# One array tile per chunk for the recurrence heads, and a re-ordered normalization at the end of the first feed-forward block

## The chip, the cores and the metric

The kernel runs on 1 core of one Trainium2 chip. The metric is the device time of one execution in microseconds (us). Engines are named as in the profile: PE is TensorE (PEld its weight loads), DVE is VectorE, ACT is ScalarE, POOL is GpSimd, SP issues DMAs.

## The reference

Two layers run over 128 context tokens and 1024 latent tokens (1152 in all, D = 1024). Layer 0 is attention beside a gated convolution, then a gated ConvFFN; layer 1 is a two-way gated linear recurrence (HGRN2), then a ConvFFN. All products are fp32. What matters here:

```
xp = _layer_norm(ALPHA * xp + gt2_p * fp, ln2_g[l], ln2_b[l])     # end of each layer, the same for xs
...
z = (h @ w_in).astype(F32)                                        # next layer, h = x*(1+scale)+shift
q, i, g, f_fw, f_bw = jnp.split(z, 5, axis=-1)
...
scores = jnp.einsum('bhtk,bhsk,bhtsk->bhts', qb, kb, decay)       # per head, within a chunk
o = o_inter + jnp.einsum('bhts,bhsv->bhtv', scores, vb)
S_new = exp(b_last) * S + jnp.einsum('bhsk,bhsv->bhkv', kb * jnp.exp(b_last - b), vb)
```

So each token's row gets a mean and a variance, is normalized, scaled and shifted, and then enters the recurrence's input projection; there, each of 8 heads builds decayed keys and queries.

## The kernel before, in words

Tokens lie in 9 tiles t of 128 rows, taken from t = 8 down to 0, and in 3 chunks c of 384 columns (tiles 3c to 3c+2), taken 2, 1, 0. A product in fp32 precision is three matmuls of a high and a low half (mm3, L93 to L95): high is a rounded copy (ACT), low the remainder (value minus high).

All engines run the order in which the code is written (one manual schedule over all engines); each engine takes its instructions in that order and waits at semaphores, which the tile framework sets from what overlaps in a tile.

**End of a feed-forward block** (ffn_down, loop at L1408). For each t PE makes two halves of 12 matmuls of 512 columns into a bank pair psw. Then DVE multiplies by the gate rows (L1421), adds into y[t] and sums it (L282), ACT squares with a sum (L285). That is ln_sums; its second part, end(), is: DVE L288, POOL's power -0.5 (L289), DVE L290, ACT L291, which writes the normalized y[t]. settle(t+1) calls end() of the tile before between the two halves of tile t.

For layer 0, tail0 puts jobs into a list todo when a chunk's three tiles are normalized: 4 jobs for chunk 2, 3 for chunk 1; the fifth of these rows of work and chunk 0's are left to the start of the next layer (later0). A job is ln_out for two 128-blocks: 6 PE transposes (L320) into two banks psl, one evacuated by DVE (L328), one by ACT (L325), both into hts with scale and shift; ACT then writes the high half (L335) and DVE or POOL the low half (L336) of the next layer's input, in turn. Jobs are taken after each half of the products. The dictionary pre adds the next layer's first weights: at t = 7 two DMAs, at t = 4, 2 and 0 one split each (ACT L108, then DVE L109).

**Start of the recurrence.** PE runs the first projections (psp, 384 columns) with later0's five jobs between them (psl's role is taken by pss there).

**Heads** (L1579 on). A head's four arrays KBF, QAB, QAF, KBB of 1152 columns are one tile X. For 7 levels and 3 chunks, 21 items: mixed_keys (ACT L1624) copies km out of X for the item after; level makes 3 products per item (PE L1635, shown as 6 rows) from km and X, then multiplies parts of X in place, one half on POOL and one on DVE (both L1641), and DVE puts the scores in place by a mask (L1643). Between items, fill(n) runs steps of 3 projection matmuls for the next head. Head 7 has no next head, so there is less to fill with.

Lines that the prediction's steps touch: L282 to L291, L320 to L336, L1399 to L1426, L1446 to L1456, L108, L109, L1568 to L1573, L1583, L1592 to L1598, L1621 to L1644.

Of the kernel before, what the change touches and what calls it, by code (L numbers as in the profile page):

```python
# [80 lines left out]
def build(tc, ins, outs, consts):  # L81
# [197 lines left out]
    def ln_sums(z, p2, small, other=None, junk=None):  # L279
# [7 lines left out]
        def end():  # L287
            nc.vector.tensor_scalar(mv[:, 3:4], mv[:, 2:3], 1.0 / D, EPS, op0=ALU.mult, op1=ALU.add)  # L288
            nc.gpsimd.tensor_tensor(mv[:, 4:5], mv[:, 3:4], mhalf[:, 0:1], op=ALU.pow)  # L289
            nc.vector.tensor_tensor(mv[:, 5:6], mv[:, 1:2], mv[:, 4:5], op=ALU.mult)  # L290
            nc.scalar.activation(z, z, AF.Identity, bias=mv[:, 5:6], scale=mv[:, 4:5])  # L291
        return end
# [13 lines left out]
    def ln_affine(xn, gb, out, dst, eng=None):  # L306

        for cols, e in eng or ((slice(0, D), (nc.gpsimd, nc.gpsimd)),):
            e[0].tensor_tensor(out[:, cols], xn[:, cols], gb[:, 0, cols], op=ALU.mult)  # L309
            e[1].tensor_tensor(out[:, cols], out[:, cols], gb[:, 1, cols], op=ALU.add)  # L310
            nc.sync.dma_start(dst[:, cols], out[:, cols])

# [969 lines left out]
    def ffn_down(l, xsrc, mod_list, dw, tail, pre):  # L1282
        with ExitStack() as st:
# [114 lines left out]
            todo, behind, end = [], [], None  # L1398
            def settle(t):  # L1399

                nonlocal behind
                if end:
                    end()
# [4 lines left out]
            for t in range(NT - 1, -1, -1):  # L1408
# [6 lines left out]
                if todo:  # L1415
                    todo.pop(0)()
                products(ps[:, 1, :], gi, t, [NU - 2, NU - 1])
                if todo:
                    todo.pop(0)()
                p2 = ps.rearrange("p a b -> p (a b)")  # L1420
                nc.vector.tensor_tensor(p2, p2, rows[:, cond_of(t), :], op=ALU.mult)  # L1421
                end = ln_sums(y[t], p2, lp)
                if t in pre:
                    pre[t]()
            settle(0)
# [6 lines left out]
    def tail0(t, y, gb, x1_tile, bank, lp, todo):  # L1432
# [5 lines left out]
        if t % 3 == 0:  # L1438
# [13 lines left out]
            now = [lambda f=f: f(bank, tmp) for f in fs[:n]]  # L1452
            if c:
                todo.append(lambda: None)
            now[2:2] = [lambda: None] * (c == 2)
            todo += now  # L1456
# [36 lines left out]
    m32 = gp.tile([P, 4, NTOK], I32, tag="X", name="m32").rearrange("p a b -> p (a b)")[:, :7 * P].rearrange(  # L1493
# [33 lines left out]
    def scan_ap(X, a0, a1, c0, n, h):  # L1527
# [3 lines left out]
                       [list(base.ap[0]), [2 * h, n // (2 * h)], [(a1 - a0) * NTOK + h, 2], [1, h]])  # L1531
# [7 lines left out]
    class Head:  # L1539
# [42 lines left out]
        def begin(self):  # L1582
            self.X = persistent("X", [P, 4, NTOK])  # L1583
# [8 lines left out]
        def arrays(self, c):  # L1592
            X, fb, q, cols = self.X, self.fb, self.q[c], colsof(c)
            nc.scalar.activation(X[:, 0:4:3, cols], fb[:, :, cols], AF.Identity, bias=one, scale=-1.0)
            nc.gpsimd.tensor_tensor(X[:, QAF, cols], q, fb[:, 0, cols], op=ALU.mult)
            nc.vector.tensor_tensor(X[:, QAB, cols], q, fb[:, 1, cols], op=ALU.mult)
            kk = self.kk[c] = wtile("kk")
            nc.vector.tensor_tensor(kk, X[:, KBF, cols], X[:, KBB, cols], op=ALU.add)  # L1598
# [22 lines left out]
        def mixed_keys(self, lv, c):  # L1621
# [3 lines left out]
                           scan_ap(self.X, KBF, KBB, c * 384, 384, hh))  # L1625

        def level(self, lv, c):
            X, cols = self.X, colsof(c)
# [4 lines left out]
            for q3 in range(3):  # L1633
                c0 = c * 384 + q3 * P
# [490 lines left out]
```

## Time and profile before

| | |
|---|---|
| median of 3 runs | 3256.94 us (3255.2 to 3258.32) |
| the profiled execution | 3256.72 us, span of its instructions 3254.9 us |
| PE busy | 3136.4 us, 96% of the span |
| DVE, ACT, POOL busy | 2247.9 (69%), 1288.9 (40%), 1422.9 us (44%) |
| mean granted TensorE clock | 0.99 |

The last product of the first feed-forward block's end starts at 1448.84 us and the last of later0's transposes ends at 1537 us; the heads' items run from 1583 to 2311 us. Times within the span are us from its start. A row of the timeline is: start, duration, engine, line, operation, output from input, shapes, how many, and in brackets the idle time of the engine before it and what ended it. A row of the view of waits is: engine, tile and line that waited, for whom, and then us in total, times, longest.

### The profile page before, as it was taken

Reading aid. Unit: us, or ns where it says so; the run is one execution under the profiler, and the core shown is the slowest. Engines: PE = TensorE matmul, PEld = TensorE weight load, DVE = VectorE, ACT = ScalarE, POOL = GpSimd, SP = SyncE. Lnnn points to the kernel's source line nnn. Section 1 sums busy time; section 2 is a strip of 40 time slices with the busy share of each in tenths; the row PEclk is TensorE's granted clock in tenths of the full one; section 3 lists DMA queues with packets and bytes.
Section 4 is the critical chain, followed back from the end, with each engine's and each line's share of the span. In section 5 each row is a group of like instructions: output and inputs, shape, how many; then the busy total and the mean of one; then the engine's idle time right before and its main releaser. Section 6 shows DMA issues by size and latency. Waiting matters only on the chain. (4 is left out here: it accounts for less than half of the span.)

```text
span 3254.9 us, 48740 instructions
## 1 busy us (share of the span) xinstructions
PE 3136.4 (96%) x19231; PEld 2906.1 (89%) x19231; DVE 2247.9 (69%) x3117; ACT 1288.9 (40%) x2162; POOL 1422.9 (44%) x1011
## 2 busy tenths in 40 slices
PE   7999999899999999998999999999999999999997
PEld 5999888789999998877999999999779999998886
DVE  6778888448988976674466666655556889675356
ACT  4411998333333333115433334333443433335112
POOL 6821242335444534562244333333424545444465
PEclk9999999999999999999999999999999999999999
DMA  7142000322222335541322222211331222225452
GB/s 221 35 136 91 1 1 1 129 85 67 95 91 88 91 119 188 171 154 64 99 83 76 65 68 80 62 50 43 111 122 55 87 91 91 69 82 185 154 169 83
DMA packets 267476, 305.42 MB, mean 94 GB/s; under 512 B 19587, under 2 KB 200015, under 8 KB 267248
## 3 DMA queue, kind: packets, MB, share of 16 engines
q1 hardware_dynamic: 266160, 299.49, 29.0%
q8 instruction: 152, 2.49, 0.3%
q0 software_dynamic: 1088, 2.82, 0.3%
q14 instruction: 76, 0.62, 0.1%
HBM read 237.84 MB, written 64.42 MB: 93 GB/s over the span
## 5 line engine op out<-in xcount | busy, mean ns | idle before, releaser
L1099 POOL TENSOR_TENSOR wlo<-S,whi 128x512 fp32r<-128x512 f32 x152 | 243.1, 1613 | 251.9 <-ACT whi L1098 251.3
L109 POOL TENSOR_TENSOR wlo<-wraw,whi 128x1024 fp32r<-128x1024 f32 x78 | 198.0, 2541 | 203.4 <-ACT whi L108 203.2
L93 PE MATMUL psd<-whi,s 128*128 128x512 f32 x720 | 284.0, 394 | 0.9 <-DVE u L1243 0.9
L95 PE MATMUL psd<-whi,s 128*128 128x512 f32 x720 | 284.0, 394 | 0.0
L94 PE MATMUL psd<-wlo,s 128*128 128x512 f32 x720 | 284.0, 394 | 0.0
L1641 POOL TENSOR_TENSOR X<-X,tot 128x384 f32<-128x384 f32 x144 | 181.4, 1260 | 226.8 <-PE pss L1635 173.7
L1127 DVE SCALAR_TENSOR_TENSOR t<-u,fcw,t 128x1156 f32<-128x1156 f32 x152 | 266.2, 1768 | 13.5 <-ACT t L1122 10.8
L95 PE MATMUL psq<-T,wlo 128*128 128x290 f32 x912 | 271.0, 297 | 0.0
L94 PE MATMUL psq<-T,whi 128*128 128x290 f32 x912 | 270.5, 297 | 0.0
L93 PE MATMUL psq<-T,whi 128*128 128x290 f32 x912 | 270.3, 296 | 0.0
L1099 POOL TENSOR_TENSOR wlo<-wraw,whi 128x512 fp32r<-128x512 f32 x114 | 182.2, 1599 | 173.1 <-ACT whi L1098 157.3
L108 ACT ACTIVATE whi<-wraw 128x1024 fp32r<-128x1024 f32 x130 | 136.8, 1054 | 291.2 <-DMA wraw<-in_ffn_w_down_dram 107.0
L1098 ACT ACTIVATE whi<-S 128x512 fp32r<-128x512 f32 x152 | 92.9, 627 | 323.2 <-DVE S L1077 249.0
L1357 DVE TENSOR_TENSOR y<-y,psd 128x512 f32<-128x512 f32 x144 | 98.0, 684 | 171.9 <-PE psd L95 171.3
L213 DVE SCALAR_TENSOR_TENSOR macc<-mraw,sil,macc 128x512 f32<-128x512 f32 x182 | 191.7, 1092 | 7.1 <-DMA mraw<-in_w_mod_dram 7.1
L93 PE MATMUL psu<-h,whi 128*128 128x388 f32 (+1 forms) x504 | 175.0, 348 | 12.1 <-DVE sc L639 6.9
L1641 DVE TENSOR_TENSOR X<-X,tot 128x384 f32<-128x384 f32 x144 | 102.1, 709 | 113.1 <-PE pss L1635 75.1
L94 PE MATMUL psu<-h,whi 128*128 128x388 f32 (+1 forms) x504 | 174.4, 346 | 2.5 <-POOL h L428 2.5
L1635 PE MATMUL pss<-X,km 128*128 128x128 f32 x1008 | 153.2, 289 | 23.7 <-ACT km L1624 10.3
L93 PE MATMUL psp<-s,whi 128*128 128x384 f32 x480 | 174.7, 364 | 0.0
L95 PE MATMUL psu<-h,wlo 128*128 128x388 f32 (+1 forms) x504 | 173.2, 344 | 0.0
L94 PEld LDWEIGHTS psq<-T,whi 128*128 128x128 f32 x912 | 172.5, 189 | 0.0
(442 smaller groups left out, 10005.2 us busy)
## 6 DMA issues: line engine op xcount, KB each, us to landing
wraw<-in_ffn_w_up_dram SPq DMA_DIRECT2D x88, 512.0 KB, 3.8
mraw<-in_w_mod_dram SPq DMA_DIRECT2D x104, 256.0 KB, 2.8
sraw<-sd SPq DMA_DIRECT2D x40, 578.0 KB, 4.6
wraw<-in_ffn_w_down_dram SPq DMA_DIRECT2D x44, 512.0 KB, 4.1
sd<-t SPq DMA_DIRECT2D x36, 578.0 KB, 3.0
wraw<-in_hgrn_w_in_dram SPq DMA_DIRECT2D x40, 512.0 KB, 4.1
mraw<-in_w_mod_dram SPq DMA_DIRECT2D x28, 512.0 KB, 4.0
wraw<-in_attn_w_in_dram SPq DMA_DIRECT2D x18, 512.0 KB, 3.8
```

The source lines that it names most:

```text
L93: mm(ps, l[0], r[0], start=start, stop=False)
L94: mm(ps, l[0], r[1], start=False, stop=False)
L95: mm(ps, l[1], r[0], start=False, stop=stop)
L108: nc.scalar.activation(hi[:, :n], raw[:, :n], AF.Copy)
L109: (eng or nc.gpsimd).tensor_tensor(lo[:, :n], raw[:, :n], r32(hi[:, :n]), op=ALU.subtract)
L213: nc.vector.scalar_tensor_tensor(acc[:, cond, :], raw, sil[:, cond, k:k + 1], acc[:, cond, :], op0=ALU.mult, op1=ALU.add)
L1098: nc.scalar.activation(hi, src, AF.Copy)
L1099: nc.gpsimd.tensor_tensor(lo, src, r32(hi), op=ALU.subtract)
L1127: nc.vector.scalar_tensor_tensor(t, u[:, :, c0:c0 + HO], taps(p + NF * x)[c0], t, op0=ALU.mult, op1=ALU.add)
L1357: nc.vector.tensor_tensor(y[t][:, cols], y[t][:, cols], ps, op=ALU.add)
L1635: mm(ps[:, q3 * P:(q3 + 1) * P], km[:, q3 * P:(q3 + 1) * P], scan_ap(X, QAB, QAF, c0, P, hh), start=True, stop=True)
L1641: eng.tensor_tensor(x, x, t4[:, :, :, 1 - half].unsqueeze(3).to_broadcast([P, 2, nb, hh]), op=ALU.mult)
```

## The change

It does three things. (1) ln_sums can return its second part in two, factor (L288, L289) and apply (the rest). In settle, factor comes first, then waiting low halves, then a job's transposes and evacuations, then apply, then a weight split, then that job's high and low half. The second place for a job is after the second half of the products, where both evacuations are on ACT, the high half comes after the square, and the low half waits for the next settle. So there is one job per place, and a free place ahead of each chunk's first. The splits of t = 4, 2 and 0 move from behind the sums of tiles 4, 2 and 0 to behind apply of tiles 3, 1 and 0. (2) The low halves of these seven jobs are all on POOL. (3) X becomes three tiles X0, X1, X2 of 384 columns, one per chunk.

```diff
--- before.py
+++ after.py
@@ ln_sums @@
-    def ln_sums(z, p2, small, other=None, junk=None):
+    def ln_sums(z, p2, small, other=None, junk=None, two=False):
...
-        def end():
+        def factor():
             nc.vector.tensor_scalar(mv[:, 3:4], mv[:, 2:3], 1.0 / D, EPS, op0=ALU.mult, op1=ALU.add)
             nc.gpsimd.tensor_tensor(mv[:, 4:5], mv[:, 3:4], mhalf[:, 0:1], op=ALU.pow)
+
+        def apply():
             nc.vector.tensor_tensor(mv[:, 5:6], mv[:, 1:2], mv[:, 4:5], op=ALU.mult)
             nc.scalar.activation(z, z, AF.Identity, bias=mv[:, 5:6], scale=mv[:, 4:5])
-        return end
+        return (factor, apply) if two else lambda: (factor(), apply())
+    def ln_pair(c, xns, l, i, bank, tmp, hT, segs, k0):
+
+
+        (cond, h0, n), = segs
+        o, box = hgb[:, l, i, cond], {}
+
+        def front(alone):
+            box["t"] = t2 = tmp()[:, :768].rearrange("p (a b) -> p a b", b=384)
+            for k in (k0, k0 + 1):
+                ps = bank()
+                for q in range(3):
+                    nc.tensor.transpose(ps[:, q * P:(q + 1) * P], xns[q][:, k * P:(k + 1) * P], ident)
+                if k % 2 or alone:
+                    nc.scalar.activation(t2[:, k - k0, :], ps[:, :n], AF.Identity, bias=o[:, 1, k:k + 1],
+                                         scale=o[:, 0, k:k + 1])
+                else:
+                    nc.vector.tensor_scalar(t2[:, k - k0, :], ps[:, :n], o[:, 0, k:k + 1], o[:, 1, k:k + 1],
+                                            op0=ALU.mult, op1=ALU.add)
+
+        def high():
+            nc.scalar.activation(hT[0].ks(k0, 2, h0, n), box["t"], AF.Copy)
+
+        def low():
+            nc.gpsimd.tensor_tensor(hT[1].ks(k0, 2, h0, n), box["t"], r32(hT[0].ks(k0, 2, h0, n)), op=ALU.subtract)
+        return front, high, low
@@ ffn_down @@
-            todo, behind, end = [], [], None
+            todo, behind, end, lows = [], [], None, []
...
                 if end:
-                    end()
+                    end[0]()
+                    for f in lows:
+                        f()
+                    lows.clear()
+                    job = todo.pop(0) if todo else None
+                    if job:
+                        job[0](False)
+                    end[1]()
+                    if t + 1 in pre:
+                        pre[t + 1]()
+                    if job:
+                        job[1]()
+                        job[2]()
...
-                if todo:
-                    todo.pop(0)()
                 products(ps[:, 1, :], gi, t, [NU - 2, NU - 1])
-                if todo:
-                    todo.pop(0)()
+                job = todo.pop(0) if todo else None
+                if job:
+                    job[0](True)
                 p2 = ps.rearrange("p a b -> p (a b)")
                 nc.vector.tensor_tensor(p2, p2, rows[:, cond_of(t), :], op=ALU.mult)
-                end = ln_sums(y[t], p2, lp)
+                end = ln_sums(y[t], p2, lp, two=True)
+                if job:
+                    job[1]()
+                    lows.append(job[2])
+            settle(0)
+            for t in (1, 0):
                 if t in pre:
                     pre[t]()
-            settle(0)
@@ tail0 @@
-            now = [lambda f=f: f(bank, tmp) for f in fs[:n]]
             if c:
-                todo.append(lambda: None)
-            now[2:2] = [lambda: None] * (c == 2)
-            todo += now
+                todo += [None] + [ln_pair(c, y[3 * c:3 * c + 3], 0, 1, bank, tmp, state["h"], hsegs(c, False), 2 * a)
+                                  for a in range(n)]
@@ heads @@
-                       [list(base.ap[0]), [2 * h, n // (2 * h)], [(a1 - a0) * NTOK + h, 2], [1, h]])
+                       [list(base.ap[0]), [2 * h, n // (2 * h)], [(a1 - a0) * 384 + h, 2], [1, h]])
...
-            self.X = persistent("X", [P, 4, NTOK])
+            self.X = [persistent(f"X{c}", [P, 4, 384]) for c in range(3)]
...
-                           scan_ap(self.X, KBF, KBB, c * 384, 384, hh))
+                           scan_ap(self.X[c], KBF, KBB, 0, 384, hh))
...
-            X, cols = self.X, colsof(c)
+            X = self.X[c]
...
-                x = X[:, arrs, cols].rearrange("p a (n s r) -> p a n s r", s=2, r=hh)[:, :, :, half, :]
+                x = X[:, arrs, :].rearrange("p a (n s r) -> p a n s r", s=2, r=hh)[:, :, :, half, :]
```

The same replacement of X by X[c] stands in arrays, state_at, flip and output. Nothing on the SP queue changes its place.

**VectorE in the end of the first feed-forward block**, from the sum of tile 4 (y_12166) to the gate product of tile 3. hts is a job's evacuated transposes, h_13784 and s_13405 are low halves of the next layer's input, wlo a weight's low half, bmv the statistics of a tile. Before:

```order
L282 SCALAR_TENSOR_TENSOR y_12166,bmv<-psw,y_12166 128x1024
L284 TENSOR_SCALAR bmv<-bmv 128x1
L109 TENSOR_TENSOR wlo<-wraw,whi 128x1024
L288 TENSOR_SCALAR bmv<-bmv 128x1
L290 TENSOR_TENSOR bmv<-bmv 128x1
L328 TENSOR_SCALAR hts<-psl,hgb 128x384 x2
L336 TENSOR_TENSOR s_13405<-hts,s_13404 128x2x384
L1421 TENSOR_TENSOR psw<-psw,rows 128x1024
L282 SCALAR_TENSOR_TENSOR y_12167,bmv<-psw,y_12167 128x1024
```

With the change, the same stretch and one tile more:

```order
L282 SCALAR_TENSOR_TENSOR y_12166,bmv<-psw,y_12166 128x1024
L284 TENSOR_SCALAR bmv<-bmv 128x1
L288 TENSOR_SCALAR bmv<-bmv 128x1
L331 TENSOR_SCALAR hts<-psl,hgb 128x384
L292 TENSOR_TENSOR bmv<-bmv 128x1
L1461 TENSOR_TENSOR psw<-psw,rows 128x1024
L282 SCALAR_TENSOR_TENSOR y_12167,bmv<-psw,y_12167 128x1024
L284 TENSOR_SCALAR bmv<-bmv 128x1
L288 TENSOR_SCALAR bmv<-bmv 128x1
L292 TENSOR_TENSOR bmv<-bmv 128x1
L109 TENSOR_TENSOR wlo<-wraw,whi 128x1024
L1461 TENSOR_TENSOR psw<-psw,rows 128x1024
```

The weight split has moved from ahead of a tile's own statistics to ahead of the next tile's gate product, the evacuation of a job stands ahead of the second part of the normalization, and the low half has left this engine.

**GpSimd in the same stretch**, from the first power of -0.5 after the last whole split to the last tile's. Before:

```order
L289 TENSOR_TENSOR bmv<-bmv,mhalf 128x1 x3
L336 TENSOR_TENSOR h_13784<-hts,h_13783 128x2x384
L289 TENSOR_TENSOR bmv<-bmv,mhalf 128x1 x2
L336 TENSOR_TENSOR s_13405<-hts,s_13404 128x2x384
L289 TENSOR_TENSOR bmv<-bmv,mhalf 128x1
L336 TENSOR_TENSOR h_13784<-hts,h_13783 128x2x384
L289 TENSOR_TENSOR bmv<-bmv,mhalf 128x1
L336 TENSOR_TENSOR s_13405<-hts,s_13404 128x2x384
```

With the change:

```order
L289 TENSOR_TENSOR bmv<-bmv,mhalf 128x1 x4
L338 TENSOR_TENSOR h_13784<-hts,h_13783 128x2x384
L289 TENSOR_TENSOR bmv<-bmv,mhalf 128x1
L338 TENSOR_TENSOR h_13784<-hts,h_13783 128x2x384
L338 TENSOR_TENSOR s_13405<-hts,s_13404 128x2x384
L289 TENSOR_TENSOR bmv<-bmv,mhalf 128x1
L338 TENSOR_TENSOR s_13405<-hts,s_13404 128x2x384
L289 TENSOR_TENSOR bmv<-bmv,mhalf 128x1
L338 TENSOR_TENSOR h_13784<-hts,h_13783 128x2x384
L289 TENSOR_TENSOR bmv<-bmv,mhalf 128x1
L338 TENSOR_TENSOR h_13784<-hts,h_13783 128x2x384
L338 TENSOR_TENSOR s_13405<-hts,s_13404 128x2x384
```

Seven low halves stand there instead of four, three of them directly behind a tile's power.

**PE in the first head**, where the products of the second item (chunk 1) follow six of the projection's matmuls; the engines named are those whose semaphores the row waits for. Before:

```order
L93 MATMUL psp_14729<-h00_13783,whi_14564 128x384
L94 MATMUL psp_14729<-h10_13784,whi_14564 128x384
L95 MATMUL psp_14729<-h00_13783,wlo_14565 128x384
L1635 MATMUL pss_14735<-X_14568,km_14712 128x128 [waits Pool_49]
L1635 MATMUL pss_14735<-X_14568,km_14712 128x128 x2
```

With the change:

```order
L93 MATMUL psp_14731<-h00_13783,whi_14564 128x384
L94 MATMUL psp_14731<-h10_13784,whi_14564 128x384
L95 MATMUL psp_14731<-h00_13783,wlo_14565 128x384
L1676 MATMUL pss_14737<-X1_14569,km_14714 128x128 [waits PE_49,Activation_49]
L1676 MATMUL pss_14737<-X1_14569,km_14714 128x128 x2
```

The place is the same; the wait for GpSimd, which multiplies in chunk 2 at that time, is gone, and what is left is the wait for this chunk's own km.

## Rows read from the trace of the kernel before

**Rows 1.** The page's first part: busy time, share of the span and instructions of PE.
```profile
PE 3136.4 (96%) x19231; PEld 2906.1 (89%) x19231; DVE 2247.9 (69%) x3117; ACT 1288.9 (40%) x2162; POOL 1422.9 (44%) x1011
```
**Rows 2.** Waits of PE from 1440 to 1537 us, the end of the first feed-forward block and the start of the recurrence.
```profile
PE psl L320 <- DVE hts L328: 4.8, 2, 4.3
PE psl L320 <- ACT y L291: 3.2, 2, 2.3
PE pss L320 <- ACT psw L285: 2.0, 1, 2.0
PE pss L320 <- ACT y L291: 1.5, 1, 1.5
PE psl L320 <- ACT hts L325: 1.2, 2, 0.8
```
**Rows 3.** Busy time by stretch in the same place: length, then busy us and instructions of PE, PEld, DVE, ACT, POOL, the granted clock, DMA share, GB/s.
```profile
1470.00:1490.00 20.00, 15.10 (x74) 11.88 (x72) 9.60 (x19) 9.30 (x14) 3.47 (x4) 0.95 0.00 1
1490.00:1510.00 20.00, 16.94 (x66) 13.41 (x66) 9.42 (x17) 10.20 (x13) 4.78 (x4) 0.79 0.09 27
```
**Rows 4.** Groups of instructions by line and shape from 1449 to 1537 us: busy us, mean ns of one, idle before.
```profile
L1421 DVE TENSOR_TENSOR psw<-psw,rows 128x1024 f32<-128x1024 f32 x9 | 11.0, 1224 | 1.0 <-PE psw L95 1.0
L285 ACT ACTIVATE psw<-y,bmv 128x1024 f32<-128x1024 f32 x9 | 10.1, 1119 | 32.9 <-DVE bmv L284 32.9
L289 POOL TENSOR_TENSOR bmv<-bmv,mhalf 128x1 f32<-128x1 f32 x9 | 4.9, 543 | 43.1 <-DVE bmv L288 43.1
L336 POOL TENSOR_TENSOR h<-hts,h 128x768 fp32r<-128x768 f32 x2 | 3.7, 1852 | 8.8 <-ACT h L335 8.8
L109 DVE TENSOR_TENSOR wlo<-wraw,whi 128x1024 fp32r<-128x1024 f32 x3 | 3.7, 1226 | 6.9 <-ACT whi L108 6.9
```
**Rows 5.** The timeline around PE's longest wait in that place, one engine's rows after the other (DVE, then PE).
```profile
1481.71 0.96 DVE L336 TENSOR_TENSOR h<-hts,h 128x768 fp32r<-128x768 f32 x1 [2.22 <-ACT h L335]
...
1487.59 1.23 DVE L109 TENSOR_TENSOR wlo<-wraw,whi 128x1024 fp32r<-128x1024 f32 x1 [2.31 <-ACT whi L108]
...
1489.67 0.67 DVE L328 TENSOR_SCALAR hts<-psl,hgb 128x384 f32<-128x384 f32 x1
...
1490.40 0.90 PE L320 MATMUL psl<-ident,y 128*128 128x128 f32 x3 [4.34 <-DVE hts L328]
```
**Rows 6.** Busy time by stretch, columns as in Rows 3: one middle head's period, then the first and the second part of head 7's items.
```profile
1678.00:1777.00 99.00, 97.03 (x647) 95.71 (x647) 66.53 (x122) 39.04 (x70) 42.10 (x31) 1.00 0.26 83
2262.00:2280.00 18.00, 13.89 (x79) 12.68 (x78) 12.03 (x28) 6.72 (x13) 7.39 (x6) 0.91 0.15 51
2280.00:2312.00 32.00, 26.28 (x176) 23.11 (x174) 23.26 (x37) 12.39 (x24) 20.97 (x17) 1.00 0.32 100
```
**Rows 7.** Waits of PE from 1580 to 2262 us, heads 0 to 6.
```profile
PE pss L1635 <- ACT km L1624: 8.1, 7, 1.2
PE pss L1635 <- POOL X L1641: 3.8, 8, 1.7
PE pss L1635 <- DVE X L1641: 1.6, 5, 0.3
```
**Rows 8.** Waits of PE from 2262 to 2312 us, head 7.
```profile
PE pss L1635 <- POOL X L1641: 5.9, 6, 1.3
PE pss L1635 <- ACT km L1624: 2.3, 4, 1.1
PE pss L1635 <- DVE X L1641: 0.5, 1, 0.5
```
**Rows 9.** The view of tile X, POOL's products in it: count, duration ns min/median/max, first and last start, shapes.
```profile
L1641 POOL TENSOR_TENSOR X<-X,tot x144: 837/1254/2017, 1595.2 to 2310.2; 128x384 f32<-128x384 f32 x144
```
**Rows 10.** The timeline of PE in head 7: the last projection matmul ahead of an item's products and those products, once with a wait and once without.
```profile
2284.65 0.34 PE L95 MATMUL psp<-s,wlo 128*128 128x384 f32 x1
2286.25 0.94 PE L1635 MATMUL pss<-X,km 128*128 128x128 f32 x6 [1.26 <-POOL X L1641]
2286.94 0.42 PE L93 MATMUL psp<-s,whi 128*128 128x384 f32 x1
...
2298.37 0.34 PE L95 MATMUL psp<-s,wlo 128*128 128x384 f32 x1
2298.55 0.83 PE L1635 MATMUL pss<-X,km 128*128 128x128 f32 x6
2299.14 0.42 PE L93 MATMUL psp<-s,whi 128*128 128x384 f32 x1
```
**Rows 11.** The timeline at head 0's first item: two runs of the same five small products of two SBUF tiles on DVE, and POOL's first product in X.
```profile
1582.34 1.32 DVE L1610 TENSOR_TENSOR tot<-tot 128x192 f32<-128x192 f32 x5
1584.36 2.25 DVE L1610 TENSOR_TENSOR tot<-tot 128x192 f32<-128x192 f32 x5
...
1584.64 1.19 POOL L1641 TENSOR_TENSOR X<-X,fb 128x384 f32<-128x384 f32 x1 [18.58 <-PE pss L1635]
```
**Rows 12.** The timeline at the end of head 0: a power on POOL, POOL's next instruction, and the DVE instruction that waited for the power.
```profile
1660.63 0.86 POOL L1697 TENSOR_TENSOR ss<-ss,mhalf 128x3 f32<-128x3 f32 x1 [6.92 <-DVE ss L1696]
1661.47 0.99 POOL L1595 TENSOR_TENSOR X<-q,fb 128x384 f32<-128x384 f32 x1
...
1661.53 0.56 DVE L1699 TENSOR_TENSOR on<-pss,ss 128x384 f32<-128x384 f32 x1 [0.98 <-POOL ss L1697]
```

More of the change, by code (lines that the diff above doesn't have):

```diff
@@ L1492, in build @@
     masks = gs.tile([P, 7, P], U8, name="masks")
-    m32 = gp.tile([P, 4, NTOK], I32, tag="X", name="m32").rearrange("p a b -> p (a b)")[:, :7 * P].rearrange(
+    m32 = gp.tile([P, 4, 384], I32, tag="X0", name="m32").rearrange("p a b -> p (a b)")[:, :7 * P].rearrange(
         "p (a b) -> p a b", b=P)
@@ L1592, in arrays @@
         def arrays(self, c):
[L1593 to L1596, printed above, removed]
+            X, fb, q, cols = self.X[c], self.fb, self.q[c], colsof(c)
+            nc.scalar.activation(X[:, 0:4:3, :], fb[:, :, cols], AF.Identity, bias=one, scale=-1.0)
+            nc.gpsimd.tensor_tensor(X[:, QAF, :], q, fb[:, 0, cols], op=ALU.mult)
+            nc.vector.tensor_tensor(X[:, QAB, :], q, fb[:, 1, cols], op=ALU.mult)
             kk = self.kk[c] = wtile("kk")
-            nc.vector.tensor_tensor(kk, X[:, KBF, cols], X[:, KBB, cols], op=ALU.add)
+            nc.vector.tensor_tensor(kk, X[:, KBF, :], X[:, KBB, :], op=ALU.add)
         def totals(self, c):
@@ L1633, in level @@
             for q3 in range(3):
-                c0 = c * 384 + q3 * P
-                mm(ps[:, q3 * P:(q3 + 1) * P], km[:, q3 * P:(q3 + 1) * P], scan_ap(X, QAB, QAF, c0, P, hh),
+                mm(ps[:, q3 * P:(q3 + 1) * P], km[:, q3 * P:(q3 + 1) * P], scan_ap(X, QAB, QAF, q3 * P, P, hh),
                    start=True, stop=True)
@@ L1649, in state_at @@
                 return self.S0[:, dr, :]
-            return self.X[:, KBB if dr else KBF, t * P:(t + 1) * P]
+            return self.X[t // 3][:, KBB if dr else KBF, t % 3 * P:(t % 3 + 1) * P]
         def flip(self, dr, c):
@@ L1654, in flip @@
             for q3 in range(3):
-                t = 3 * c + q3
                 nc.tensor.transpose(pt[:, q3 * P:(q3 + 1) * P],
-                                    self.X[:, KBB if dr else KBF, t * P:(t + 1) * P], ident)
+                                    self.X[c][:, KBB if dr else KBF, q3 * P:(q3 + 1) * P], ident)
             kb = wtile("kb")
@@ L1681, in output @@
             po = pst()
-            X, V = self.X, shared["V"]
+            X, V = self.X[c], shared["V"]
             for q3 in range(3):
                 t = 3 * c + q3
-                cols = slice(t * P, (t + 1) * P)
+                cols = slice(q3 * P, (q3 + 1) * P)
                 o = po[:, q3 * P:(q3 + 1) * P]
```

## The prediction

> **What bounds it now.** The page's first part comes first: PE is busy for 3136.4 of 3254.9 us [rows 1], so that only stretches in which PE stands, or runs at its lower clock, can give time back. The view of PE's waits, taken by stretch, then shows which of them lie where the diff works. The reader is to see three places. From 1440 to 1537 us PE stands 12.7 us in all (4.8 + 3.2 + 2.0 + 1.5 + 1.2), each time ahead of transposes [rows 2]; the timeline shows the longest of these waits, 4.34 us, with VectorE's rows ahead of it [rows 5]; and right behind it the clock granted to TensorE averages 0.79 over 20 us [rows 3], a mixture of its two levels, 2.4 and 1.2 GHz, after PE had stood. In heads 0 to 6 PE waits 5.4 us for POOL's and DVE's products in X and 8.1 us for km [rows 7]. In head 7, which has little to fill with, it waits 5.9 and 0.5 us for X and 2.3 us for km [rows 8]. A middle head is dense, 97.03 us busy in 99 [rows 6]; head 7 is not, 13.89 in 18 and 26.28 in 32.
>
> **End of the feed-forward block, wait by wait.** The largest, 4.8 us, is for the evacuation L328. In the timeline it stands on VectorE behind the weight split L109, which itself idled 2.31 us for ACT's half; L328 then runs 0.67 us and PE resumes [rows 5]. Afterwards the evacuation stands ahead of both the second part of the normalization and the split. I take all 4.8 us as gone. The 3.2 us for y are waits of a job's transposes that came one after the other in the same pause; a job now stands at least 12 matmuls later, some 2.4 us (74 PE instructions take 15.10 us [rows 3], 0.20 each), against a longest wait of 2.3: gone too. Of the 1.2 us for ACT's evacuation nothing is left if ACT keeps up; the three evacuations that move from DVE to ACT cost it some 0.67 us each, if they take there what they take on DVE [rows 5], against 32.9 us that it stands idle ahead of L285 alone [rows 4], so no path.
>
> The 1.5 us behind y at the stage's end goes, as tile 0's L288 no longer stands behind the split of 1.226 us [rows 4]. The 2.0 us for L285 ahead of the last transposes grow instead: the split that stood behind tile 2's sums stands now behind tile 1's, ahead of tile 0's gate product L1421, on the one chain that has no product left to cover it. It is 1.226 us on DVE [rows 4]; all of it on the path gives 3.2 us, none 2.0. I take 3.0, as its ACT half also runs there. **This is what is late next.**
>
> **The lows on GpSimd.** Three lows that DVE did in 0.96 us [rows 5] go to POOL, where one takes 1.852 us [rows 4]; POOL idles 43.1 us ahead of L289 alone there, so its time as such is covered. But the lows of the three jobs from the second place stand directly behind a power of -0.5 (tiles 4, 3 and 1), and VectorE's next instruction is a product of two SBUF inputs that waits for that power. No row shows this pair. The nearest: the same five small SBUF products on DVE take 1.32 us alone and 2.25 us when a POOL product of 1.19 us begins among them [rows 11], 0.93 us longer; so the two engines do hold each other up. And after a power POOL's next instruction begins before the DVE instruction that waited for the power does, at 1661.47 against 1661.53 us [rows 12]; so POOL gets in first. The bounds of such a hold are 0 and the whole low, 1.85 us, three times. I take the whole, because most of that POOL product is found again on DVE. At tiles 4 and 3 most of it lies beside the 24 matmuls of the next tile; I leave 1.5 us for late banks. At tile 1 the split, the gate product of tile 0 and so the end of the chain stand behind it: 3.0 + 1.85 = 4.8. PE's waits are then 6.3 us instead of 12.7: **6.4 us gained** (9.7 without the hold, where 3.0 are left).
>
> The Trainium skill ("SBUF — State Buffer", "SBUF: two separate sides") calls the port that the two engines share an exclusive lock for a whole instruction, which also binds a VectorE operation with two SBUF inputs against GpSimd; by it the hold is 1.85 us each time, the value taken above, and the trace agrees so far as 0.93 us of 1.19 show [rows 11]. The same skill ("Perfetto Trace Analysis", "Optimizing Scalar/DVE Operations") warns that offloading between these two engines might not help, a rule against this part of the change.
>
> **The clock.** In 1490 to 1510 us PE is busy 16.94 us at 0.79 [rows 3]: at full clock 16.94 x 0.21 = 3.6 us less. It fell after a wait of 4.34 us; the gaps left by the sum are at most that long in one place, at the stage's end. I give back half, **1.8 us**; the ends are 0 and 3.6. The stage gives 8.2 us; its ends are 6.4 and 9.7 + 3.6 = 13.3.
>
> **Heads 0 to 6.** One tile per chunk takes away the waits of a chunk's products, of its km and of its multiplications for another chunk's. I let the 5.4 us for X [rows 7] go whole: what POOL multiplies in its own chunk was begun two items before. The 8.1 us for km are seven waits of 8.1 / 7 = 1.16 us, one a head; km keeps its place on ACT and the waits stay. A stall costs more than its wait. In head 7 an item's products start 1.60 us behind the start of the last projection matmul with a recorded wait of 1.26, and 0.18 us behind it without one [rows 10]: 1.60 - 0.18 - 1.26 = 0.16 more; and the next projection comes 0.69 against 0.59 us behind the products' start, 0.10 more. With 8 + 5 stalls at 0.26 us that is 3.4. **8.8 us**; the lower end 4, if half of the waits turns into one for km.
>
> **Head 7.** To be had: 5.9 + 0.5 for X, and of km's 2.3 all but one wait as in the other heads, 1.16, so 7.5; with about 10 stalls at 0.26, 10.1. Against all of it speaks POOL: 7.39 + 20.97 = 28.4 us busy for 21 items in 50 us [rows 6], a product in X 1.254 us at the median and up to 2.017 [rows 9], and PE with nothing to wait for would pass the items in some 40 us (13.89 + 26.28). POOL would be at 70%, uneven, with its side work in the same queue. I take 60%, **6.1 us**, with 2.5 and 10.1 as ends. The clock of 0.91 over 13.89 us [rows 6] costs 1.25 us; half of it, **0.6**.
>
> Splitting the tile and merging its access patterns change no duration that I can see; the cover is only that X's operations have the same number of elements. Were each of POOL's 144 products longer by 5%, it would be 0.06 us a time, hidden in heads 0 to 6, and inside head 7's ends.
>
> **The sum.** 8.2 + 8.8 + 6.1 + 0.6 = 23.7 us; 3256.72 (the profiled execution, 0.2 us under the median of 3256.94) - 23.7 = **3233.0 us**.
>
> **Rivals.** *VectorE is not held by GpSimd* in the new pair: with no pause but the last one the clock comes back whole, the stage gives 13.3 us and the time is 3227.9. For it: no row has just this pair, and the 0.93 us [rows 11] could be five short delays. Against it: the 0.93 us. Chance 0.22.
>
> *GpSimd becomes head 7's bound, and half the waits of the other heads turn into km's*: 8.2 + 4 + 2.5 = 14.7, 3242.0. For it: the long products of 2.017 us [rows 9], and that POOL is the releaser of most of head 7's waits. Against it: POOL idles 30% there. Chance 0.22.
>
> *One tile per chunk changes nothing*, as where PE waited for another chunk's product the own one came no sooner: only the stage's 8.2 us, 3248.5. Against it: in the order the wait for POOL at such a place is gone, and what replaces it is km alone. Chance 0.05.
>
> *Slower*: the holds at tiles 4, 3 and 1 leave PE a gap in each tile, and TensorE stays at 1.2 GHz from about 1470 to 1510 us, where the clock has dropped already after one such gap. PE's work there is 15.10 x 0.95 + 16.94 x 0.79 = 27.7 us at full speed [rows 3]; at 1.2 GHz throughout it takes 27.7 us more, against 4.4 before. Then 6.4 + 8.8 + 6.7 - 23.3 = -1.4: 3258.1. It decides from some 26 us of full-speed work at the low level; to end slower by over 0.2% the low level would also have to reach 6 us of work past 1510. Against it: the pauses it needs are hidden by 24 matmuls in two of three places, and the 4.34 us pause goes. Chance 0.05, with 0.02 of it below and 0.03 over the bound.
>
> **Numbers.** The forecast has 0.46. The range takes its ends (a stage of 6.4 and heads 4 + 2.5 would be 3243.8; a stage of 13.3 and all of head 7 would be 3223.3), the first two rivals and not the last two: 3224 to 3246, about 8 in 10. A measurement of this kernel can tell about 0.2%, 6.5 us, from no change. Faster than 3250.4: forecast, two rivals and nearly all of the third, 0.93; within 0.2%: 0.04; slower 0.03.
>
> **What would show it.** In the stage: no wait of PE for DVE's hts; a wait for L285 of 3 to 5 us ahead of the last transposes; L292, which did its work in a fraction of a microsecond, ending up to 1.85 us behind its power where a low stands there; the last transposes near 1528.6 instead of 1536.8. In the heads: PE's waits for POOL's and DVE's products in X nearly gone, the seven waits of 1.16 for km still there, a middle head's period some 1.2 us shorter, head 7 shorter by 6 to 7. I am wrong if PE's waits in the heads only change their name, if the clock falls in new places, or if the wait ahead of the last transposes is over 5 us.

## The result, and the profile after

The changed kernel takes 3228.11 us (median of 4 runs, 3226.79 to 3231.56) against 3257.18 us; the ratio is 0.9914 with an interval of 0.9898 to 0.9930. A second set of runs of it gave 3228.40 us and 0.9916 (0.9903 to 0.9930). That is 29 us; 23.7 were forecast, 3233.0 us, in a range of 3224 to 3246.

The waits of PE from 1440 to 1531 us, in the profile after. The columns are those of [rows 2].

```profile
PE pss L348 <- ACT psw L285: 4.7, 1, 4.7
PE psl L326 <- ACT hts L328: 2.3, 1, 2.3
PE psw L93 <- DVE y L1385: 0.9, 1, 0.9
```

Where [rows 2] had eight waits and 12.7 us ahead of transposes there are two and 7.0. The third row is no part of this: the same wait of 0.9 us stands in the profile of before, ahead of the first product of this stage (the one that starts at 1448.84 us, where the last group of products begins), and isn't among [rows 2]. The wait for hts on VectorE is gone; the one for L285 has grown from 2.0 to 4.7.

Waits of PE in heads 0 to 6 (1570 to 2250 us) and then, behind the dots, in head 7 (2250 to 2284 us):

```profile
PE pss L1676 <- ACT km L1666: 8.0, 7, 1.1
PE psm L1696 <- ACT V L1614: 1.5, 6, 0.3
...
PE pss L1676 <- ACT km L1666: 3.6, 6, 1.2
```

No row names POOL's or DVE's products in X any more ([rows 7, 8] had four, 11.8 us together); in heads 0 to 6 the seven waits of 1.15 us for km have stayed as they were, while in head 7 the waits for km grew from 2.3 us in four to 3.6 us in six. The waits of 0.3 us for V stood in the heads before as well. One more row of head 7 belongs to the profile before and isn't in [rows 8], a wait of the same products for which the view names no engine; it is gone too:

```profile
PE pss L1635 <- issue: 1.0, 1, 1.0
```

Busy time by stretch in the profile after, columns as in [rows 3]; the fourth row is a middle head's period, the last one head 7's items.

```profile
1470.00:1490.00 20.00, 20.00 (x100) 16.42 (x100) 12.78 (x23) 12.88 (x18) 6.19 (x6) 1.00 0.00 1
1490.00:1510.00 20.00, 17.65 (x87) 14.41 (x86) 11.69 (x17) 11.89 (x18) 8.04 (x7) 1.00 0.37 128
1510.00:1530.00 20.00, 15.26 (x89) 14.79 (x88) 10.38 (x19) 13.37 (x23) 5.47 (x6) 0.91 0.38 132
1750.00:1848.00 98.00, 96.60 (x650) 95.94 (x649) 69.86 (x121) 38.06 (x69) 35.78 (x29) 1.00 0.26 82
2250.00:2284.00 34.00, 31.05 (x209) 29.07 (x210) 32.67 (x49) 16.43 (x29) 22.37 (x20) 1.00 0.32 100
```

PE is busy without a gap from 1470 to 1490, at full clock. Some of the lower level is left, later: 0.91 in 1510 to 1530, a stretch that had 1.00 before; it holds the end of the wait of 4.7 and what follows it.

To see where the time came from, marks that both kernels pass are set against each other. First the changed kernel: PE's tile psw in this stage and its last transposes (durations, then first and last start), the last power of head 6, and PE's first instruction behind head 7's items that waited.

```profile
L93 PE MATMUL psw<-whi,s x72: 388/396/484, 1451.1 to 1508.3; 128*128 128x512 f32 x72
...
L348 PE MATMUL pss<-ident,y x30: 270/272/421, 1517.1 to 1530.3; 128*128 128x128 f32 x30
...
2244.26 0.85 POOL L1737 TENSOR_TENSOR ss<-ss,mhalf 128x3 f32<-128x3 f32 x1 [4.42 <-DVE ss L1736]
...
2285.93 0.55 PE L1696 MATMUL psm<-ident,X 128*128 128x128 f32 x3 [0.28 <-ACT V L1614]
```

The same marks in the kernel before:

```profile
L93 PE MATMUL psw<-whi,s x72: 387/396/777, 1448.8 to 1517.3; 128*128 128x512 f32 x72
...
L320 PE MATMUL pss<-ident,y x30: 270/273/331, 1523.4 to 1536.8; 128*128 128x128 f32 x30
...
2261.89 0.85 POOL L1697 TENSOR_TENSOR ss<-ss,mhalf 128x3 f32<-128x3 f32 x1 [4.45 <-DVE ss L1696]
...
2312.12 0.55 PE L1656 MATMUL psm<-ident,X 128*128 128x128 f32 x3 [0.29 <-ACT V L1572]
```

| stretch | before | after | gained | forecast |
|---|---|---|---|---|
| stage: first psw to last transposes | 88.0 | 79.2 | 8.8 | 8.2 |
| heads 0 to 6: to the last power of head 6 | 725.1 | 714.0 | 11.1 | 8.8 |
| head 7: to the transposes of X | 50.2 | 41.7 | 8.6 | 6.7 |

Together 28.5 us. The spans of these two executions differ by less, 3254.9 - 3229.8 = 25.1. The stage of the changed kernel began 2.2 us later, ahead of any changed instruction: up to 230 us TensorE had been granted 0.97 in that execution and 0.99 in the one before. Another 1.1 us went behind head 7. In the second profile of the changed kernel the stage begins at 1449.15 and the span is 3225.6. So two executions of one kernel differ by 4.2 us of span, 1.9 of it ahead of the stage. That is part of the uncertainty of every comparison of medians below; the lengths between marks repeat better, the stage's 79.2 us and the 714.0 of heads 0 to 6 to 0.1 us in both profiles.

### The profile page after: what moved, and what is told of

Its sections match the earlier page's. It is cut to its first block, busy times and chain, and to the rows that moved or that the text cites. A ratio compares the mean times of both kernels' runs of the same rounds, so it can differ in the third digit from the quotient of the medians.

```text
span 3229.8 us, 48748 instructions
## 1 busy us (share of the span) xinstructions
PE 3131.4 (97%) x19231; PEld 2909.9 (90%) x19231; DVE 2264.6 (70%) x3111; ACT 1284.4 (40%) x2165; POOL 1414.8 (44%) x1014
## 3 DMA queue, kind: packets, MB, share of 16 engines
q1 hardware_dynamic: 266160, 299.49, 29.2%
## 5 line engine op out<-in xcount | busy, mean ns | idle before, releaser
L109 POOL TENSOR_TENSOR wlo<-wraw,whi 128x1024 fp32r<-128x1024 f32 x78 | 197.3, 2533 | 206.2 <-ACT whi L108 206.1
L1155 DVE SCALAR_TENSOR_TENSOR t<-u,fcw,t 128x1156 f32<-128x1156 f32 x152 | 264.8, 1760 | 13.8 <-ACT t L1150 11.1
L1682 POOL TENSOR_TENSOR X<-X,tot 128x384 f32<-128x384 f32 x144 | 169.3, 1176 | 225.3 <-PE pss L1676 212.4
L108 ACT ACTIVATE whi<-wraw 128x1024 fp32r<-128x1024 f32 x130 | 136.8, 1054 | 289.6 <-DMA wraw<-in_ffn_w_down_dram 118.8
L93 PE MATMUL psu<-h,whi 128*128 128x388 f32 (+1 forms) x504 | 176.6, 351 | 11.6 <-DVE sc L667 6.5
L1682 DVE TENSOR_TENSOR X<-X,tot 128x384 f32<-128x384 f32 x144 | 111.6, 775 | 88.0 <-PE pss L1676 85.8
L93 PE MATMUL psp<-h,whi 128*128 128x384 f32 x480 | 172.2, 359 | 0.0
```

What stands on the lines that cost most here:

```text
L93: mm(ps, l[0], r[0], start=start, stop=False)
L108: nc.scalar.activation(hi[:, :n], raw[:, :n], AF.Copy)
L109: (eng or nc.gpsimd).tensor_tensor(lo[:, :n], raw[:, :n], r32(hi[:, :n]), op=ALU.subtract)
L1155: nc.vector.scalar_tensor_tensor(t, u[:, :, c0:c0 + HO], taps(p + NF * x)[c0], t, op0=ALU.mult, op1=ALU.add)
L1682: eng.tensor_tensor(x, x, t4[:, :, :, 1 - half].unsqueeze(3).to_broadcast([P, 2, nb, hh]), op=ALU.mult)
```

## The experiments

Eleven runs follow. The unit is the changed kernel's 3228.4 us unless the kernel before is named; ratios are to the kernel before, which took 3257.2 to 3258.1 us beside them.

**The changed kernel again** (no edit).

> The changed kernel itself, for a second profile and as the base of the runs beside it: 3228 us, between 3226 and 3231. In the stage (the products of 512 columns to the last transposes of the start of the recurrence) PE stands about 7 us in two waits, 4.7 for L285 and 2.3 for ACT's hts, whether or not the clock falls elsewhere.

3228.40 us; waits of 4.74 and 2.35 us in the stage. The clock had not fallen early on this time, and the two waits and the length of the stage, 79.2 us, are the same to 0.1 us.

**The two halves of the change by themselves.** Here X in three tiles without the new order of the stage:

```
-            self.X = persistent("X", [P, 4, NTOK])
+            self.X = [persistent(f"X{c}", [P, 4, 384]) for c in range(3)]
```

> Only the second half of the change: three array tiles, one per chunk, and the first feed-forward block's end as before. Theory (the two halves act on separate stretches and add up): PE's waits for products in X in heads 0 to 7 nearly vanish, the seven waits of 1.15 us for km stay, and the heads give 18.9 us: 3238 us, ratio 0.994. The stage keeps its 12.7 us of waits. Rival (the stage's earlier end or the clock after it carries part of the heads' gain): under 15 us.

3237.16 us, ratio 0.9943 (0.9931 to 0.9955): 20.1 us faster than before. PE's waits for X and km in the heads are km's alone, 11.6 us, and heads 0 to 6 take 714.0 us between the marks, as in the changed kernel. The stage keeps 11.7 of its 12.7 us of waits, the one of 4.3 among them, and its length (87.6 us).

Then the rest of the change, without these lines:

> Only the first half of the change: the re-ordered normalization, with X one tile as before. Theory: the stage gives 8 to 9 us (waits of PE from 12.7 to about 7, and the clock that fell after the long wait): 3248.5 us, ratio 0.9973; together with the run of the other half the sum of the whole change. VectorE's L292 takes 1.8 us in three places. Rival (most of the gain was in the heads and the stage only shifted waits): 3253 or more.

3250.04 us, ratio 0.9976 (0.9967 to 0.9985): 7.2 us. The stage has the changed kernel's two waits, 4.74 and 2.35 us, and L292 takes 1.79, 1.79 and 1.80 us; head 7 has the waits of [rows 8]. The stage is 79.5 us long. 20.1 + 7.2 = 27.3 of the 29 us: the halves act on separate stretches and add up within the spread of executions, and the heads have over two thirds of it.

**L292 with one streamed input.** The same product, with the power as a per-partition scalar:

```
-            nc.vector.tensor_tensor(mv[:, 5:6], mv[:, 1:2], mv[:, 4:5], op=ALU.mult)
+            nc.vector.tensor_scalar(mv[:, 5:6], mv[:, 1:2], mv[:, 4:5], None, op0=ALU.mult)
```

> The changed kernel with one instruction written otherwise: L292 multiplies the negative mean by the power as a per-partition scalar (tensor_scalar) in place of a product of two tiles; the same number, one streamed input. Theory A (GpSimd's low holds VectorE because L292 has two inputs in SBUF): L292 takes 0.16 us everywhere, also right behind a low's start; PE's wait of 2.3 falls to about 0.5 and the one of 4.7 to about 2.9; 3.5 us faster than the changed kernel, 3224.5. Theory B (GpSimd's low holds any VectorE instruction that reads SBUF, or L292 waits for something else): L292 still 1.8 us in three places and the time is the changed kernel's, 3228.

3224.95 us (3224.89 to 3225.15), 3.45 us faster, and the stage is 75.8 us long in place of 79.2, 3.4 less: theory A. In the changed kernel the timeline shows tile 3's end as follows (VectorE, then GpSimd):

```profile
1491.30 0.15 DVE L288 TENSOR_SCALAR bmv<-bmv 128x1 f32<-128x1 f32 x1 [1.41 <-ACT psw L285]
1492.17 1.79 DVE L292 TENSOR_TENSOR bmv<-bmv 128x1 f32<-128x1 f32 x1 [0.72 <-POOL bmv L289]
1496.28 1.22 DVE L109 TENSOR_TENSOR wlo<-wraw,whi 128x1024 fp32r<-128x1024 f32 x1 [2.32 <-ACT whi L108]
...
1491.60 0.54 POOL L289 TENSOR_TENSOR bmv<-bmv,mhalf 128x1 f32<-128x1 f32 x1 [0.65 <-DVE bmv L288]
1492.12 1.83 POOL L338 TENSOR_TENSOR s<-hts,s 128x768 fp32r<-128x768 f32 x1
```

GpSimd begins the low half 0.05 us ahead of L292, and L292, one element wide, ends with it. With one streamed input, at the same place:

```profile
1489.27 0.21 DVE L292 TENSOR_SCALAR bmv<-bmv 128x1 f32<-128x1 f32 x1 [0.72 <-POOL bmv L289]
...
1488.70 0.54 POOL L289 TENSOR_TENSOR bmv<-bmv,mhalf 128x1 f32<-128x1 f32 x1 [2.14 <-DVE bmv L288]
1489.21 1.85 POOL L338 TENSOR_TENSOR s<-hts,s 128x768 fp32r<-128x768 f32 x1
```

The low starts first again and takes as long, and L292 is done in 0.21 us, as in every other place of this kernel (0.05 more than the other form takes alone). The waits of PE in this kernel's stage:

```profile
PE pss L348 <- ACT psw L285: 3.2, 1, 3.2
PE psw L93 <- DVE y L1385: 0.9, 1, 0.9
PE psl L326 <- ACT hts L328: 0.7, 1, 0.7
```

3.2 and 0.7 us in place of 4.7 and 2.3. Both waits had the hold in them: at tile 1 that of the last chain, and at tile 3 the other, by way of L293, the split (L108, L109) and tile 2's gate product, which stand behind L292. The edit changes the operation as well as the number of streamed inputs, and its second factor is still read from SBUF; no run separates the two, so that what is shown is that this form isn't held.

**The three lows on VectorE.**

```
                     for f in lows:
-                        f()
+                        f(nc.vector)
```

> The changed kernel with the three low halves that stand directly behind a power put on VectorE again (0.96 us each), in the same place of the order. Theory (what costs is that L292 is held for the 1.79 us of GpSimd's low): L292 takes 0.16 us, VectorE has 0.96 us more ahead of it in three places; PE's waits fall by about 0.8 us each, the time by 1 to 2 us, 3226.5. Rival (the move to GpSimd was worth its hold, since VectorE is short there): slower than the changed kernel by 1 us or more.

3228.59 us: the median shows no difference. L292 is down to 0.16 us in all places, the waits are 4.4 and 1.3 us, 1.3 less together where the theory had 1.6, and the stage is 77.9 us long, 1.3 shorter. That is the theory's direction, too small for the medians to tell. Moving these three lows to GpSimd gained nothing as long as L292 had two streamed inputs: what VectorE was spared, it lost by being held.

**The split of tile 2's turn behind the last apply.**

```
-                    if t + 1 in pre:
+                    if t + 1 in pre and t + 1 != 2:
                         pre[t + 1]()
...
-            for t in (1, 0):
+            for t in (2, 1, 0):
```

> The changed kernel with the weight split that stood ahead of tile 0's gate product (behind apply of tile 1) moved behind apply of tile 0. Theory (this split lengthens the last chain by its 1.23 us on VectorE and partly ACT's 1.04 behind the held L292): PE's wait of 4.7 us ahead of the last transposes falls to between 2.4 and 3.6, and the time by 1 to 2 us, 3226.5. Rival (the chain is set by the held L292 and the square on ACT, the split lies beside them): 4.7 stays and the time too. Second rival: the split is needed soon behind and makes a new wait of about 1 us in the projections.

3229.98 us, not faster by the median; the interval is the changed kernel's (0.9903 to 0.9930). The waits of PE in its stage:

```profile
PE psl L326 <- ACT hts L328: 2.4, 1, 2.4
PE psp L93 <- ACT whi L108: 1.4, 1, 1.4
PE pss L348 <- ACT psw L285: 1.2, 1, 1.2
PE psw L93 <- DVE y L1385: 0.9, 1, 0.9
PE psp L95 <- DVE wlo L109: 0.7, 1, 0.7
```

The wait of 4.7 falls to 1.2 us, by more than the theory had, so the split did lie on the last chain; 2.1 us of it come back as waits of the projections for the same split's halves: the second rival, with twice its size. In this profile the stage is 76.7 us long, 2.5 shorter, with a granted clock of 1.00 where the changed kernel had 0.91; the medians, with executions from 3227.8 to 3232.8, show nothing of that.

**The first key copy of a head ahead of sT's.**

```
-        hd.mixed_keys(*items[0])
...
+            nh.mixed_keys(0, 2)
             nh.diagonal(0)
```

> The changed kernel with the first key copy of each head (level 0, chunk 2) issued ahead of the copy of the last scores into sT on ScalarE. Theory (the 1.15 us wait of each head is ScalarE's order alone): the seven or eight waits of 1.15 us for km go, each with a restart of about 0.27: 8 x 1.4 = 11 us faster than the changed kernel, 3217. Rival (PE would then wait for the copy itself, or for the array that it reads): a wait of 0.5 us or more remains at each place, gain under 5 us.

3219.31 us, ratio 0.9881 (0.9868 to 0.9895), 9.1 us faster. Heads 0 to 6 have no wait for km any more and take 704.1 us between the marks, 9.9 less, 1.41 for each wait of 1.15. So these seven waits, which the change left standing, were ScalarE's order alone. The eighth was not: in head 7 the wait ahead of the first item is gone, but the fourth item now waits 1.40 us for a copy that waits for VectorE's product in X, and 3.2 us of waits for km are left there.

**These three edits together**, and then without the later split:

> The changed kernel with three of these edits together: L292 with one streamed input, the split behind tile 0's apply, and the early key copy. Theory (they act on separate waits): PE's wait ahead of the last transposes about 1.7 us, the other of the stage about 0.5, no 1.15 us waits for km; 3.5 + 1.2 + 11 = 15.7 us faster than the changed kernel: 3212. Rival (the gains overlap or the stage's waits turn into new ones in the projections): 3216 or more.

> The changed kernel with two of the three edits: L292 with one streamed input and the early key copy, the split left ahead of tile 0's gate product. Theory (their gains, measured singly as 3.45 and 9.1 us, lie in separate stretches; the later split only turned one wait into waits of the projections): 3228.4 - 12.5 = 3215.9, as with all three. Rival (the later split does help once the hold is gone): 3217 or more.

3215.92 (ratio 0.9870, 0.9857 to 0.9884) and 3216.71 us (0.9876, 0.9862 to 0.9889). All three together give 12.5 us where 15.7 were expected: the rival's number. The later split made the same 2.1 us of waits in the projections again, and the key copy alone had given 9.1 where 11 stood in the sum. Without the split 3.45 + 9.1 = 12.5 us were expected and 11.7 measured; the two times do not differ beyond their intervals. Both beat the changed kernel by some 12 us, and the two edits, of one line and of four, are enough for it. What is left ahead of the last transposes is 0.95 us with all three and 3.21 without the later split.

**X in one tile, with the chunk as outermost dimension.**

```
-            self.X = [persistent(f"X{c}", [P, 4, 384]) for c in range(3)]
+            xx = persistent("X", [P, 3, 4, 384])
+            self.X = [xx[:, c] for c in range(3)]
```

> The changed kernel with the heads' arrays in one tile again, but with the chunk as the outermost dimension (128 x 3 x 4 x 384), so that a chunk's operands lie side by side and no two chunks' ranges interleave. Theory (the waits came from ranges that interleave, not from the number of tiles): no waits of PE for products in X, the changed kernel's time, 3228.4. Rival (a tile is followed as a whole): the waits of before come back, 19 to 20 us slower, 3248.

3229.57 us (0.9915, 0.9902 to 0.9929), the changed kernel's time; no wait of PE names a product in X. It is the layout, not the number of tiles: in 128 x 4 x 1152 the ranges of two chunks' operands interleave.

**Both halves of the products in X on VectorE.**

```
-                eng = nc.vector if half else nc.gpsimd
-                eng.tensor_tensor(x, x, t4[:, :, :, 1 - half]...
+                nc.vector.tensor_tensor(x, x, t4[:, :, :, 1 - half]...
```

> The changed kernel with both halves of the heads' products in X (L1682) on VectorE. Theory (the two engines cannot work on two SBUF inputs at the same time, so a half of 0.56 us on VectorE and one of 0.85 on GpSimd take 1.41 together as they stand, and two on VectorE 1.12): no VectorE instruction in the heads is held any more by a product in X, VectorE gets 0.56 us more per item, PE's waits in heads 0 to 6 do not grow, and the time is within 2 us of the changed kernel's 3228.4. Rival (the two halves do run side by side, and VectorE, at about 66% in the heads, comes to 80% and late): PE waits for products in X again, 3233 or more.

3239.58 us (0.9949, 0.9935 to 0.9962), 11.2 us slower: the rival's number, by another cause. From head 2 on nothing is lost: a head's period is 97.4 us as in the changed kernel, and although VectorE does GpSimd's half as well, it is busy for only 2 to 4 us more of it (71.2 against 67 to 69; 484.55 us in the 679 from 1583 on): most of the time that it now works on that half it had spent being held. The time goes in heads 0 and 1, which take 6.4 and 4.5 us more and where GpSimd has four products of 128x1024 (L306) each in its queue. In the changed kernel's second profile they stand behind the head's last product in X and run at 1632 and 1728 us; here nothing stands ahead of them, and they begin at 1571 and 1677, as soon as their data is there, ahead of head 0's first items and amid head 1's (VectorE's rows, then GpSimd's, in head 1):

```profile
1677.27 3.00 DVE L211 TENSOR_SCALAR macc<-mraw,sil 128x512 f32<-128x512 f32 x2
1680.19 3.40 DVE L109 TENSOR_TENSOR wlo<-wraw,whi 128x1024 fp32r<-128x1024 f32 x1
1683.52 5.37 DVE L1681 TENSOR_TENSOR X<-X,fb 128x384 f32<-128x384 f32 x2
1688.81 0.57 DVE L1683 COPY_PREDICATED sT<-masks,pss 128x384 f32<-128x384 uint8 x1
1689.28 1.01 DVE L1681 TENSOR_TENSOR X<-X,tot 128x384 f32<-128x384 f32 x2
...
1677.40 11.07 POOL L306 TENSOR_TENSOR rx<-rx,gb 128x1024 f32<-128x1024 f32 x4 [10.41 <-DMA rx<-xh]
```

Two products in X take 5.37 us during L306 and 1.01 behind it; a split takes 3.40 in place of 1.22. PE waits 4.8 us for km in head 0 and 2.7 in head 1 behind such stretches.

## Why the prediction was right, and where it was off

**End of the feed-forward block: the waits went as forecast, the last one by luck.** The wait for VectorE's hts is gone, and VectorE is held for 1.79, 1.79 and 1.80 us in just the three places named, behind the powers of tiles 4, 3 and 1. The wait ahead of the last transposes is 4.7 us where 4.8 stood in the sum, but the parts of that sum were mis-sized: 2.0 for the chain, 1.0 for the split that now stands ahead of tile 0's gate product, 1.85 for the hold. The runs show all four cases: 4.74 us with split and hold, 3.21 without the hold, 1.20 with the split out of the way, 0.95 without either (the run of three edits). So the chain alone is 1.0 us, the split costs 2.3 without the hold and 3.5 behind it, and the hold 1.5 with the split and 0.3 without. What the working missed on the split stands in VectorE's last row of tile 3's end above, and at tile 1 alike: ahead of its own 1.22 us VectorE idles 2.32, until ScalarE has done L293 and the split's L108. The two are 3.5 us, what the wait falls by when the split moves. A chain taken 1.0 us too long made up for a split taken 1.3 too short.

The whole low was taken as the price of a hold, and L292 shows it; one streamed input gives 3.45 us back, where the working had 3.3 in waits and the runs show 3.2. The other late banks were put at 1.5 us and cost 2.3: tile 3 was thought to be covered by 24 matmuls, but tile 4's split stands behind tile 3's held L292, too, and with it the evacuation of the next job. The clock gave back more than the half that was taken: PE's 15.26 us at 0.91 cost 1.4 us, against 3.6 and, from 1470 to 1490 us at 0.95, another 0.8 before. So 5.7 us of waits and some 2.9 of clock make nearly all of the stage's 8.8, where 6.4 and 1.8 were taken. That the clock fell in a new place was named as a sign of being wrong; it did, in 1510 to 1530 us, and the sign was too strict, for the fall was smaller than the one that went.

**The clock as a rival.** TensorE did not stay at 1.2 GHz from 1470 to 1510 us: 1.00 was granted there. What was left was the stretch behind the longest wait. (The 4.4 us of that rival's sum are 4.3 by its own rows.)

**Heads 0 to 6: the mechanism right, the size too small.** The term that was mis-sized is the count of stalls, 13 places and 5.4 us; 8.8 us were taken and 11.1 measured. The view of waits doesn't list all of them: heads 2 to 5 had one more each, with a wait under 0.15 us, and head 0 two with a wait under 0.05, none of which is in [rows 7]. In the kernel before, the timeline shows the one of head 2 so:

```profile
1785.74 0.34 PE L95 MATMUL psp<-s,wlo 128*128 128x384 f32 x1
1786.22 1.00 PE L1635 MATMUL pss<-X,km 128*128 128x128 f32 x6
1786.97 0.43 PE L93 MATMUL psp<-h,whi 128*128 128x384 f32 x1
```

and in the changed kernel at the same place so:

```profile
1774.68 0.34 PE L95 MATMUL psp<-s,wlo 128*128 128x384 f32 x1
1774.86 0.88 PE L1676 MATMUL pss<-X,km 128*128 128x128 f32 x6
1775.49 0.43 PE L93 MATMUL psp<-h,whi 128*128 128x384 f32 x1
```

0.48 us pass from the last projection to the products in place of 0.18, and 0.75 to the next projection in place of 0.63: 0.42 us, with no wait in brackets. Four times 0.42 and, by the same comparison, 0.32 and 0.28 us in head 0 are 2.3 us; 8.8 + 2.3 = 11.1 us is what was measured. The stalls that were counted cost what was worked out, a wait and about 0.26 us: head 6, with one wait of 0.26, is 0.53 us shorter, head 1, with two waits of 0.57 together, 1.10.

**Head 7: the waits for X right, km and the bound not.** It gave 8.6 us (9.3 in the second profile); 6.7 were taken, 60% of what was to be had and half of the clock. The share of 60% was a choice without a row. All waits for X went, and with them the one of 1.0 us that the sum didn't have, but km's did not fall to one: they grew by 1.3 us. Waits 9.7 - 3.6 = 6.1 us, six stalls fewer at 0.26 and the clock's 1.25 (1.00 was granted there afterwards) are 8.9, near what was measured. GpSimd, which was expected to be nearly the bound, is no more than two thirds busy, 22.37 of 34 us; the engine that is full is VectorE, 32.67 of 34. Of the five waits for km behind the first, three (1.9 us) stand behind other work on ScalarE (weight splits, a table load) and two (0.6 us) behind VectorE's products in X, which last up to 1.49 us there where the shortest lasts 0.54. No run shows that this holding costs head 7 time: with both halves of the products on VectorE it is as long, 40.8 us between the marks against 41.7 and 40.9. (GpSimd's products in X are 168, not 144: [rows 9] has those with tot, and 24 have fb.)

**The rivals.** The time lies on the number of the first, 3227.9, but that rival was wrong: VectorE is held. The number came out by the heads, which gave 4.2 us more than forecast. A time that agrees with a rival is no evidence for it; the durations of L292 decided. The second rival, half of the other heads' waits turned into km's, is refuted by the seven waits that stayed at 8.0 us; in head 7 a part of it came true, 1.3 us. That the tiles by chunk do nothing is refuted by the half of the change that was run alone.

Not settled: how much of the 29 us of the medians is the clock in stretches that no edit touches; the marks give 28.5 in one profile and 8.8 + 11.1 + 9.3 = 29.2 in the other. Nor why the clock falls behind a wait in one execution and not in another: see the last section.

## What to carry to other kernels

Where engines wait for each other's work on different parts of one array, look at whether the parts' address ranges interleave: putting the part in the outermost dimension removed every such wait of TensorE here, worth 20 us, for no instruction more. Work moved to GpSimd was not free for VectorE: a short product released together with a long one of GpSimd was held for all of it, until it was written with one streamed input. A weight split on a chain costs what its engine idles ahead of it too, not its own time alone. And a view of waits has a floor: count stalls by the distance between neighbours' starts as well.

## What the runs showed of the hardware

A VectorE product of one column with two inputs in SBUF lasted 1.79 us in place of 0.16 when a GpSimd product of 1.83 us had begun 0.05 us earlier; the same product with its second factor as a per-partition scalar lasted 0.21. The Trainium skill ("SBUF — State Buffer", "SBUF: two separate sides") names two SBUF inputs as what binds a VectorE operation against GpSimd, and by that rule the trace agrees, to the end of the instruction.

One streamed input alone is no licence, though. Of two 128x512 tensor_scalar operations (L211) in the last run, the first, begun 0.13 us ahead of GpSimd's L306, lasted 0.47 us and the second, begun 0.26 us behind its start, 2.61. The same section binds a VectorE operation in its 2-port mode as well; no run here shows which mode an instruction took, so that this case stays open.

When GpSimd's instructions followed each other within 0.1 us, VectorE finished one instruction for each of them. The two products in X lasted 2.7 us each there, where they take 0.55. In head 0 five small products of two SBUF tiles lasted 9.72 us beside four GpSimd products in place of 1.32 (VectorE's rows, then GpSimd's):

```profile
1571.07 9.72 DVE L1652 TENSOR_TENSOR tot<-tot 128x192 f32<-128x192 f32 x5
...
1581.49 1.32 DVE L1652 TENSOR_TENSOR tot<-tot 128x192 f32<-128x192 f32 x5
...
1570.91 9.63 POOL L306 TENSOR_TENSOR rx<-rx,gb 128x1024 f32<-128x1024 f32 x4 [14.09 <-DMA rx<-xh]
```

Equal waits did not bring equal clocks. Behind the same wait of 3.21 us ahead of the last transposes, and with the same waits ahead of it in the stage, TensorE was granted 0.91 over the 20 us from 1505 to 1525 in the run with one streamed input and 1.00 in the run of that edit with the early key copy; the stages are 75.8 and 74.4 us long.
